# A two-layer hybrid trunk on one core: a list scheduler's engine orders, mLSTM beside RWKV and the output projection, adaLN units moved, sub-layer boundaries by token halves

## The chip, the core and the metric

One Trainium2 chip, one of its cores. The time is device microseconds of one execution of the whole program, a median over runs; smaller is better. The engines named below are PE (TensorE; PEld is its weight load), DVE (VectorE), ACT (ScalarE), POOL (GpSimd) and SP (SyncE, which here issues nearly all DMAs).

## The reference

Two layers with a token mixer and a SwiGLU feed-forward each, for 256 tokens of width 2048 (feed-forward width 5632), all in float32. Each of the four sub-layers computes

```
x <- LayerNorm(ALPHA * x + (1 + gate(c)) * f(x * (1 + scale(c)) + shift(c)))
```

where shift, scale and gate are products of the one conditioning vector `c` with an "adaLN" matrix (2048 x 6144 for each sub-layer). f is, in order:

- layer 0, mixer "ab": one input projection, then eight mLSTM heads (two groups of four) and sixteen RWKV-7 heads (four batches of four), concatenated, then an output projection;
- layer 0, feed-forward: `silu(h Wg) * (h Wu)`, then `Wd`;
- layer 1, mixer "cd": one input projection, then retention and gated DeltaNet (GDN) heads, concatenated, then an output projection;
- layer 1, feed-forward.

RWKV and GDN need the inverse of a small triangular matrix for each head and chunk; mLSTM has a convolution, gates, a weighted score matrix and a norm for each head.

## The kernel before, in words

**Weights.** Nearly every weight is read from HBM once, in units of 1 MB (`raw`, three buffers, issued by SP). Float32 products are made of three float32r matmuls: ACT rounds half a unit into `hi` (L340), DVE subtracts to get `lo` (L341), and PE adds hi·h, lo·h and hi·(rest of h) into a PSUM bank (L360, L361, L362). A unit is four slices of 128 input rows by 512 outputs, so it is 4 slices x 2 token halves (t=0 and t=1, 128 tokens each) x 3 = 24 matmuls of 128x512. `product` (L347 on) runs the units of one block of 512 outputs into two PSUM banks, one for each token half, tag `g`.

**adaLN.** There are 192 `ada_unit`s, 48 for each sub-layer: 1 MB read through the same three `raw` buffers, and one DVE instruction that multiplies by silu(c) and sums along the row (L292). `fill(rate)` puts some of them behind each weight unit of the stages, up to a limit. When a sub-layer's 16 gate columns are there, `gate_rows` (L314) spreads them over all partitions: for each of 16 column blocks a float32 matmul of a broadcast column with the identity (L320, two records each in the profile), and four ACT copies; four times in the program.

**Stages.** `first_products` (the first 164 us) makes the RWKV low-rank columns and three blocks beside 32 adaLN units. `rwkv` runs four batches (`rwkv_batch`, `rwkv_front`, then `rwkv_heads` with `inverses`, then `rwkv_out`), and after each batch issues further blocks of the input projection, which fill PE while DVE works at the heads. The eight blocks that belong to mLSTM (6 to 13) are not used at once: `put_by` copies them out of PSUM (ACT, L705) and stores them in HBM, and `mlstm_group` fetches them later. After RWKV's last batch mLSTM group 0 and then group 1 run, then `mix_out` (the output projection, two halves of four blocks, with `residual` between), then `norm`, `ffn(0)`, `mixer_cd`, `mix_out`, `norm`, `ffn(1)`, `last_norm`.

**Boundaries.** At the end of a sub-layer the last block's banks are multiplied by the gate, added to the residual, and summed (`last_sum`: L483, L484, L485, for each token half), `norm_scales` (L493 to L505) turns the sums into mean and 1/sigma by some twelve DVE instructions of one column, DVE normalises (L522), PE transposes (L527), ACT scales and shifts (L530), and DVE splits (L390, L391) into the next activation `h`. The last unit of the last block has its matmuls ordered by token half (`by_t`), nothing else has.

**What sets the order.** The tile framework's scheduler takes instructions by program order, with offsets: weight loads and splits are 2000 places ahead, the inverses 4000, the norm 3000. Each engine then runs its instructions in that fixed order.

## Time and profile before

| | |
|---|---|
| time of three runs | 2883.45, 2884.39, 2894.77 us; median 2884.39 |
| profiled execution | 2886.5 us, its span 2884.8 us, so 1.7 us lie outside the span |
| mean granted TensorE clock | 0.970 |
| first matmul | 33.8 us; last matmul's end about 2866.3 us |
| first_products | 0 to 164 us |
| RWKV, four batches | 164 to 603 us |
| mLSTM, two groups | 603 to 686 us |
| output projection and norm | 686 to 786 us |
| feed-forward 0 | 786 to 1535 us |
| mixer cd with its output projection | 1535 to 2124 us |
| feed-forward 1 and the last norm | 2124 to 2884.8 us |

The table by stage in the prediction has, for each stretch, its length, the busy time of each engine with its number of records in brackets, the mean granted TensorE clock, the share of time that the DMA engines were busy, and GB/s. A busy PE at a clock of 0.5 does half the work, so idle time and clock have to be read together.

### The profile page before, as it was taken

Reading aid. Unit: us, or ns where it says so; the run is one execution under the profiler, and the core shown is the slowest. Engines: PE = TensorE matmul, PEld = TensorE weight load, DVE = VectorE, ACT = ScalarE, POOL = GpSimd, SP = SyncE. Lnnn points to the kernel's source line nnn. Section 1 sums busy time; section 2 is a strip of 40 time slices with the busy share of each in tenths; the row PEclk is TensorE's granted clock in tenths of the full one; section 3 lists DMA queues with packets and bytes.
Section 4 is the critical chain, followed back from the end, with each engine's and each line's share of the span. In section 5 each row is a group of like instructions: output and inputs, shape, how many; then the busy total and the mean of one; then the engine's idle time right before and its main releaser. Section 6 shows DMA issues by size and latency. Waiting matters only on the chain.

```text
span 2884.8 us, 33590 instructions
## 1 busy us (share of the span) xinstructions
PE 2699.7 (94%) x12746; PEld 2216.1 (77%) x12746; DVE 2035.7 (71%) x3255; ACT 1260.7 (44%) x1663; POOL 73.8 (3%) x88
## 2 busy tenths in 40 slices
PE   3699999987899999999998999999989999999997
PEld 2577788775788888888886778787778888888886
DVE  7888878845876557767758798886876545557556
ACT  2264444435454444444445544344444444443442
POOL 0000000000000000000000010101000000000000
PEclk9799999987999999999999999999999999999998
DMA  9876656632577668867855775667656656656553
GB/s 365 352 270 246 247 187 257 250 123 74 203 259 290 249 228 299 302 229 274 300 196 204 277 280 211 239 252 263 222 194 241 239 192 236 236 219 235 193 218 131
DMA packets 112906, 683.79 MB, mean 237 GB/s; under 512 B 12644, under 2 KB 16872, under 8 KB 35048
## 3 DMA queue, kind: packets, MB, share of 16 engines
q1 hardware_dynamic: 110152, 676.92, 64.1%
q10 hardware_dynamic: 2592, 4.72, 0.4%
q8 instruction: 100, 1.64, 0.2%
q14 instruction: 62, 0.51, 0.0%
HBM read 668.49 MB, written 13.11 MB: 236 GB/s over the span
## 4 chain that ended last, share of the span: by engine, by line
PE 58%; DVE 8%; DMA 4%; issue 1%; ACT 1%; POOL 0%; POOLq 0%; DVEq 0%; ACTq 0%
PE g L361 18%; PE g L362 18%; PE g L360 18%; DVE lo L341 3%; DMA raw<-ada 2%; DVE raw L292 2%; DMA raw<-gu 1%; ACT hi L340 1%; PE m L578 1%; DMA raw<-w_cd 1%; DMA t<-x 1%; PE m L527 0%; PE c L320 0%; PE m L642 0%; PE m L649 0%
## 5 line engine op out<-in xcount | busy, mean ns | idle before, releaser
L341 DVE TENSOR_TENSOR lo<-raw,hi 128x1024 fp32r<-128x1024 f32 (+2 forms) x848 | 1024.2, 1213 | 650.0 <-ACT hi L340 647.5
L340 ACT ACTIVATE hi<-raw 128x1024 fp32r<-128x1024 f32 (+2 forms) x848 | 885.0, 1049 | 1182.4 <-PE g L362 949.5
L360 PE MATMUL g<-hi,h 128*128 128x512 f32 (+3 forms) x2352 | 923.1, 394 | 85.7 <-ACT hi L340 81.0
L361 PE MATMUL g<-lo,h 128*128 128x512 f32 (+3 forms) x2352 | 926.1, 394 | 9.9 <-DVE lo L341 9.6
L362 PE MATMUL g<-hi,h 128*128 128x512 f32 (+3 forms) x2352 | 921.4, 392 | 0.0
L360 PEld LDWEIGHTS g<-hi,h 128*128 128x128 f32 x2352 | 447.3, 191 | 181.2 <-ACT hi L340 85.3
L361 PEld LDWEIGHTS g<-lo,h 128*128 128x128 f32 x2352 | 448.5, 191 | 108.9 <-DVE lo L341 19.9
L362 PEld LDWEIGHTS g<-hi,h 128*128 128x128 f32 x2352 | 447.6, 190 | 88.4 <-issue 3.2
L292 DVE SCALAR_TENSOR_TENSOR raw<-raw,silu_c 128x2048 f32<-128x2048 f32 x176 | 403.1, 2290 | 31.1 <-DMA raw<-ada 30.5
L360 PE MATMUL g<-hi,a 128*128 128x512 f32 x960 | 376.1, 392 | 2.0 <-ACT hi L340 1.1
L361 PE MATMUL g<-lo,a 128*128 128x512 f32 x960 | 375.6, 391 | 2.5 <-DVE lo L341 2.4
L362 PE MATMUL g<-hi,a 128*128 128x512 f32 x960 | 375.7, 391 | 0.0
L361 PEld LDWEIGHTS g<-lo,a 128*128 128x128 f32 x960 | 180.8, 188 | 40.9 <-DVE lo L341 4.0
L360 PEld LDWEIGHTS g<-hi,a 128*128 128x128 f32 x960 | 180.9, 188 | 40.3 <-ACT hi L340 1.6
L362 PEld LDWEIGHTS g<-hi,a 128*128 128x128 f32 x960 | 180.9, 188 | 37.2
L947 DVE SCALAR_TENSOR_TENSOR f<-c,cols_sb,f 128x253 f32<-128x253 f32 (+2 forms) x120 | 53.5, 475 | 13.4 <-ACT f L945 13.1
L530 ACT ACTIVATE t<-m,affine 128x128 f32<-128x128 f32 x96 | 35.0, 474 | 29.9 <-PE m L527 26.4
L1141 POOL TENSOR_SCALAR s<-cons_sb,log_alpha 128x128 f32<-128x128 f32 x16 | 18.1, 1144 | 1065.9 <-DVE log_alpha L1085 895.3
L403 ACT ACTIVATE t<-t,affine 128x256 f32<-128x256 f32 x16 | 8.7, 588 | 76.4 <-DVE affine L301 76.4
L292 DVE SCALAR_TENSOR_TENSOR a<-a,silu_c 128x2048 f32<-128x2048 f32 x16 | 36.6, 2287 | 0.4
L527 PE MATMUL m<-cons_sb,y 128*128 128x128 f32 x96 | 16.9, 319 | 18.4 <-DVE v L495 18.4
L527 PEld LDWEIGHTS m<-cons_sb,y 128*128 128x128 f32 x96 | 13.3, 167 | 23.1 <-issue 20.2
(391 smaller groups left out, 1990.1 us busy)
## 6 DMA issues: line engine op xcount, KB each, us to landing
raw<-ada SPq DMA_DIRECT2D x176, 1024.0 KB, 5.1
raw<-gu SPq DMA_DIRECT2D x176, 1024.0 KB, 4.9
raw<-dn SPq DMA_DIRECT2D x88, 1024.0 KB, 4.8
raw<-w_cd SPq DMA_DIRECT2D x60, 1024.0 KB, 5.1
raw<-w_ab SPq DMA_DIRECT2D x56, 1024.0 KB, 5.5
a<-ada SPq DMA_DIRECT2D x16, 1024.0 KB, 9.6
raw<-o_ab SPq DMA_DIRECT2D x16, 1024.0 KB, 4.9
raw<-o_cd SPq DMA_DIRECT2D x16, 1024.0 KB, 4.8
```

The source lines that it names most:

```text
L292: v.scalar_tensor_tensor(w[:], w[:], 1.0, self.sc[:], ALU.mult, ALU.mult, accum_out=m[:, i:i + 1])
L340: nc.scalar.activation(hi[:, :2 * n], ws, AF.Copy)
L341: nc.vector.tensor_tensor(lo[:, :2 * n], ws, hi[:, :2 * n], ALU.subtract)
L360: mm(o, ah, wh, start=first, stop=False)
L361: mm(o, ah, wl, start=False, stop=False)
L362: mm(o, al, wh, start=False, stop=stop and k == 3)
L403: nc.scalar.activation(h32[:, j, :], x[:, j, :], AF.Identity, bias=self.ab[:, 16 + k:17 + k], scale=self.ab[:, k:k + 1])
L527: nc.tensor.transpose(b[:, P * j:P * j + P], y[t][:, P * k:P * k + P], self.ident)
L530: nc.scalar.activation(h32[:, j, :], b[:, P * j:P * j + P], AF.Identity, bias=self.ab[:, 16 + k:17 + k], scale=self.ab[:, k:k + 1])
L578: nc.tensor.transpose(b[:, P * k:P * k + P], gs[:, t, P * k:P * k + P], self.ident)
L947: v.scalar_tensor_tensor(o[:, d:T], z[:, 0:T - d], self.col(wname, c + 3 - d), o[:, d:T], ALU.mult, ALU.add)
L1141: nc.gpsimd.tensor_scalar(L[:], sl, self.gl[:, t, 4 * g + j:4 * g + j + 1], None, ALU.mult)
```

## The change

1. **A list scheduler in the kernel** (`Plan`, 330 new lines). After the whole program is recorded, it works out each instruction's dependences, gives each a cost by a small table (written in the kernel, with a model of the clock and of one DMA stream), runs a list schedule over the five engines with the old priorities as tie-breaker and the pools' buffer counts as limits, and pins each engine to the order that came out (`impose`), by dependences without a semaphore.
2. **mLSTM beside other work.** `rwkv_heads`, `inverses` and `mlstm_group` become generators. Group 0 is stepped along beside RWKV's last batch (`beside`). Group 1 is handed into `mix_out` as `side` and stepped beside the first half of the output projection; its four blocks (10 to 13) are made there and used straight from PSUM (`direct`), so they are neither stored nor fetched: ACT's `put_by` stores go from 18 to 10.
3. **adaLN units moved.** By stage, before and after: start 32 and 32; RWKV to the first output projection 48 and 48; feed-forward 0 48 and 60; mixer cd 48 and 36; feed-forward 1 16 and 16. After a norm eight weight units pass without one (four before). The scale and shift table keeps all four sub-layers apart.
4. **Gate without PE.** `gate_rows` no longer uses PE or ACT. When a sub-layer's gate is complete, a DMA writes its 128x16 columns transposed into HBM (2048 elements of four bytes), and a second DMA reads the 8 KB row back to all partitions (1 MB). The program has 64 PE matmuls fewer (11775 instead of 11839).
5. **Boundaries by token halves.** The last two units (mixers) or three units (feed-forwards) of a sub-layer's last block run all matmuls of t=0, then all of t=1; the first three units of the next sub-layer do the same. Their split halves live in other pools (`a8`, `q4`, `zt`) so that all are held at once. `norm` takes t=0 to the end before t=1, at a priority of 12000; the normalisation moves from DVE to ACT. `last_norm` goes by halves too.
6. **Small.** Three DVE instructions instead of four for each Newton step of `rsqrt`; in `conv`, `shifted` and `scaled_into` both ACT instructions of a pair are issued before DVE's.

```diff
-    def gate_rows(self):
-        gate = self.y8([P, D])
-        for n in range(4):
-            b = self.bank("c")
-            for j in range(4):
-                k = 4 * n + j
-                self.nc.tensor.matmul(b[:, P * j:P * j + P], self.g1[:, k:k + 1].to_broadcast([P, P]), self.ident, start=True, stop=True)
-            self.nc.scalar.activation(gate[:, 512 * n:512 * n + 512], b[:], AF.Copy)
+        if i == 47:
+            v.scalar_tensor_tensor(self.g1[:], m[:, 32:48], 1.0, self.cols[:, ob + 32:ob + 48], ALU.add, ALU.add)
+            self.gate_row = self.dram.tile([KT, P], F32, name=self.name("gate_row"))
+            nc.sync.dma_start(self.gate_row[:].rearrange("k p -> p k"), self.g1[:])
+
+    def gate_rows(self, room, sub):
+        self.ada(max(0, 48 * sub + 48 - self.ada_next))
+        gate = room([P, D])
+        self.nc.sync.dma_start(gate[:], self.gate_row[:].rearrange("k p -> (k p)").unsqueeze(0).to_broadcast([P, D]))
         return gate
...
+        groups = [(0, head)] + [(i, ("ss",)) for i in range(len(head), m - len(tail))] + [(m - len(tail), tail)]
+        for first, homes in groups:
+            units = range(first, first + len(homes))
+            parts = {i: self.split(srcs[i], n, homes=home) for i, home in zip(units, homes)}
+            if len(homes) == 1:
+                order = [(i, r, t) for i in units for r in range(2) for t in range(NT)]
+            else:
+                order = [(i, r, t) for t in range(NT) for i in units for r in range(2)]
...
+        with self.tc.high_priority(offset=12000):
+            for t, g in ((0, None), (0, 0), (0, 1), (0, 2), (0, 3), (1, None), (1, 0), (1, 1), (1, 2), (1, 3)):
+                if g is None:
+                    self.last_sum(y, banks, 3, stats, [t])
+                    mean, r = self.norm_scales(stats[t])
...
-            if out:
-                out()
-            if i < 4:
-                out = self.rwkv_heads(B)
+            side = beside(i)
+            for _ in self.rwkv_heads(B):
+                next(side, None)
...
-        rate = 48.0 / 80 if l == 0 else 16.0 / 60
+        rate = 64.0 / 84 if l == 0 else 16.0 / 40
...
-        k.mixer_cd(h, 48.0 / 60)
+        k.mixer_cd(h, 32.0 / 44)
...
+        plan = Plan(tc, tc.nc, 250)
+        plan.prepare(0)
+        order, _ = plan.run([x.bass_priority for x in plan.ins])
+        plan.impose(order)
```

What this makes of the order is shown at three places of PE's list. Rows are PE's instructions in order; `xN` is that many of one kind in a row, `g` banks are those of weight products, `m` and `c` banks those of small matmuls.

**First place, the inversions of RWKV's third batch.** Before (L632, L642, L649, L656 are the inversion's matmuls):

```order
L632 MATMUL m_2754<-cons_sb,y_2700 128x128 x4
L362 MATMUL g_3898<-hi_4021,h_674 128x512
L360 MATMUL g_3898<-hi_4021,h_674 128x512
L361 MATMUL g_3898<-lo_4022,h_674 128x512
L362 MATMUL g_3898<-hi_4021,h_674 128x512
L360 MATMUL g_4059<-hi_4063,h_140 128x512
L361 MATMUL g_4059<-lo_4064,h_140 128x512
L362 MATMUL g_4059<-hi_4063,h_140 128x512
L360 MATMUL g_4059<-hi_4063,h_140 128x512
L361 MATMUL g_4059<-lo_4064,h_140 128x512
L362 MATMUL g_4059<-hi_4063,h_140 128x512
L632 MATMUL m_2761<-cons_sb,y_2700 128x128 x4
```

With the change (L1002, L1013, L1020, L1027 are the same matmuls):

```order
L1002 MATMUL m_2750<-cons_sb,y_2696 128x128 x4
L1002 MATMUL m_2757<-cons_sb,y_2696 128x128 x4
L1013 MATMUL m_2763<-y_2696,a_2642 128x64 x4
L1013 MATMUL m_2768<-y_2696,a_2642 128x64 x4
L1161 MATMUL c_3480<-f_3473,cons_sb 128x256
L1020 MATMUL m_2763<-P_2773,y_2696 128x64 x4
L1020 MATMUL m_2768<-P_2775,y_2696 128x64 x4
L1027 MATMUL m_2787<-cons_sb,y_2696 128x128 x4
L1027 MATMUL m_2793<-cons_sb,y_2696 128x128 x4
L1013 MATMUL m_2799<-y_2696,a_2642 128x64 x4
```

Before, weight matmuls (the `g` rows) stand between the inversion's steps; with the change none does for 78 rows, from this batch's first inversion step on, through its heads and into the next batch's first steps (the first ten are shown).

**Second place, mLSTM group 0.** Before, from the second head on (L1000 to L1004 make the weights of a head, L1014 and L1015 its scores, L1041 to L1043 its output):

```order
L1014 MATMUL m_4642<-y_4547 128x256
L1015 MATMUL m_4642<-y_4547 128x128
L1041 MATMUL m_4646<-q_4624,t_4638 128x129
L1042 MATMUL m_4646<-q_4624,t_4638 128x129
L1043 MATMUL m_4646<-q_4624,t_4638 128x129
L1000 MATMUL m_4660<-cons_sb,s_4657 128x256
L1001 MATMUL m_4660<-cons_sb,log_f 128x128
L1002 MATMUL m_4660<-minus_m,cons_sb 128x256
```

With the change, in RWKV's last batch (L1027 is that batch's inversion, L1377 to L1381 are an mLSTM head's weights, L1391 and L1392 its scores):

```order
L1027 MATMUL m_3828<-cons_sb,y_3729 128x128 x4
L1027 MATMUL m_3834<-cons_sb,y_3729 128x128 x4
L1377 MATMUL m_3844<-cons_sb,s_3841 128x256
L1378 MATMUL m_3844<-cons_sb,log_f 128x128
L1379 MATMUL m_3844<-minus_m,cons_sb 128x256
L1380 MATMUL m_3844<-cons_sb,s_3841 128x128
L1381 MATMUL m_3844<-minus_m,cons_sb 128x128
L1391 MATMUL m_3854<-y_3628 128x256
L1392 MATMUL m_3854<-y_3628 128x128
L704 MATMUL g_4599<-hi_4645,h_319 128x512
L705 MATMUL g_4599<-lo_4646,h_319 128x512
L706 MATMUL g_4599<-hi_4645,h_319 128x512
```

Before, one mLSTM head follows another with no weight matmul between; with the change a head stands between the inversion's steps and weight matmuls of the last batch.

**Third place, the boundary from the first mixer to feed-forward 0.** Before (L527 is the norm's transpose):

```order
L361 MATMUL g_5705<-lo_5747,a_5102 128x512
L362 MATMUL g_5705<-hi_5746,a_5102 128x512
L527 MATMUL m_5828<-cons_sb,y_5121 128x128 x4
L360 MATMUL g_5959<-hi_5963,h_5782 128x512
L361 MATMUL g_5959<-lo_5964,h_5782 128x512
L362 MATMUL g_5959<-hi_5963,h_5782 128x512
```

With the change (L884 is the transpose):

```order
L705 MATMUL g_5643<-lo_5659,a_5229 128x512
L706 MATMUL g_5643<-hi_5658,a_5229 128x512
L884 MATMUL m_5742<-cons_sb,y_4211 128x128 x4
L884 MATMUL m_5757<-cons_sb,y_4211 128x128 x4
L884 MATMUL m_5772<-cons_sb,y_4211 128x128 x4
L704 MATMUL g_5899<-q_5903,h_5710 128x512
L705 MATMUL g_5899<-q_5904,h_5710 128x512
L706 MATMUL g_5899<-q_5903,h_5710 128x512
```

In both, no work of another kind stands between the last weight matmul and the first transpose; with the change three of the first half's four transposes stand together, and the 24 matmuls ahead of them all belong to t=1.

More of the change, by code (lines that the diff above doesn't have):

```diff
@@ L364, in product, with part @@
-    def product(self, srcs, n, acts, ada=0.0, by_t=False):
+    def part(self, w, i, n, act, t, bank, start, stop):
+        mm = self.nc.tensor.matmul
+        hi, lo = w
+        ts = slice(P * t, P * t + P)
+        o = bank[:, :n]
+        for j in range(2):
+            k = 2 * i + j
+            ah, al = act[:, 0, k, ts], act[:, 1, k, ts]
+            wh, wl = hi[:, n * j:n * j + n], lo[:, n * j:n * j + n]
+            mm(o, ah, wh, start=start and k == 0, stop=False)
+            mm(o, ah, wl, start=False, stop=False)
+            mm(o, al, wh, start=False, stop=stop and k == 3)
@@ L366, in product, with unit @@
+    def unit(self, src, n, act, banks, start, stop, ahead=2000):
+        parts = self.split(src, n, ahead)
+        for i in range(2):
+            for t in range(NT):
+                self.part(parts[i], i, n, act, t, banks[t], start, stop)
+    def product(self, srcs, n, acts, ada=0.0, head=(), tail=()):
         banks = [self.bank("g") for _ in range(NT)]
         m = len(srcs)
-        for i, s in enumerate(srcs):
-            self.unit(s, n, acts[i], banks, i == 0, i == m - 1, by_t=by_t and i == m - 1)
-            self.fill(ada)
+        groups = [(0, head)] + [(i, ("ss",)) for i in range(len(head), m - len(tail))] + [(m - len(tail), tail)]
[4 more added lines that the diff above has]
+                order = [(i, r, t) for i in units for r in range(2) for t in range(NT)]
+            else:
+                order = [(i, r, t) for t in range(NT) for i in units for r in range(2)]
+            for i, r, t in order:
+                self.part(parts[i][r], r, n, acts[i], t, banks[t], i == 0, i == m - 1)
+            for _ in units:
+                self.fill(ada)
@@ L507, in norm_scales @@
-        return out
-    def norm(self, y, stats, sub):
+        mv, r = self.tiny([P, 2]), self.tiny([P, 1])
+        v.bn_aggr(mv[:], stats[:].rearrange("p (c s) -> p c s", s=6))
+        x, x4, x16, t, u = (self.tiny([P, 1])[:] for _ in range(5))
+        v.tensor_scalar(x, mv[:, 1:2], LN_EPS, None, ALU.add)
+        v.tensor_single_scalar(t.bitcast(I32), x.bitcast(I32), 1, ALU.logical_shift_right)
+        v.tensor_scalar(u.bitcast(I32), t.bitcast(I32), -1.0, float(0x5F3759DF), ALU.mult, ALU.add)
@@ new lines, in norm, with group @@
+        scales = {}
+        def group(t, g):
+            s, ts = slice(512 * g, 512 * g + 512), slice(P * t, P * t + P)
+            mean, r = scales[t]
+            nc.scalar.activation(y[t][:, s], y[t][:, s], AF.Identity, bias=mean, scale=r)
+            b = self.bank()
+            h32 = self.t2([P, 4, P])
+            for j in range(4):
+                k = 4 * g + j
+                nc.tensor.transpose(b[:, P * j:P * j + P], y[t][:, P * k:P * k + P], self.ident)
+            for j in range(4):
+                k = 4 * g + j
+                nc.scalar.activation(h32[:, j, :], b[:, P * j:P * j + P], AF.Identity, bias=self.ab[:, sub + 1, 16 + k:17 + k],
+                                     scale=self.ab[:, sub + 1, k:k + 1])
+                if j % 2:
+                    self.into(acts[g], ts, h32[:, j - 1:j + 1, :], slice(j - 1, j + 1))
@@ new lines, in norm @@
+        with self.tc.high_priority(offset=12000):
+            for t, g in ((0, None), (0, 0), (0, 1), (0, 2), (0, 3), (1, None), (1, 0), (1, 1), (1, 2), (1, 3)):
+                if g is None:
+                    self.last_sum(y, banks, 3, stats, [t])
+                    mean, r = self.norm_scales(stats[t])
+                    off = self.tiny([P, 1])
+                    v.scalar_tensor_tensor(off[:], mean, -1.0, r, ALU.mult, ALU.mult)
+                    scales[t] = off[:], r
+                else:
+                    group(t, g)
@@ L567, in ffn @@
                 u0 = (l * NFB + j) * 8
-                banks = self.product([gu[u0 + i] for i in range(4)], 512, h, rate)
+                banks = self.product([gu[u0 + i] for i in range(4)], 512, h, rate, head=HEAD if j == 0 else ())
                 gs = self.q4([P, NT, 512])
@@ L584, in ffn @@
             if third == 1:
-                self.gate = self.gate_rows()
+                self.gate = self.gate_rows(self.y8, sub)
             for n in range(4):
                 u0 = l * 44 + d0 + n * m
-                banks = self.product([dn[u0 + i] for i in range(m)], 512, a, 0.0, by_t=third == 2 and n == 3)
+                banks = self.product([dn[u0 + i] for i in range(m)], 512, a, 0.0, tail=FFN_TAIL if third == 2 and n == 3 else ())
                 if third == 0:
@@ L1326, in product @@
             at[0] += KG
-            return self.product([w[u + i] for i in range(KG)], 512, h, rate)
+            return self.product([w[u + i] for i in range(KG)], 512, h, rate, head=() if u else HEAD)
         def gates():
```

582 lines of the change are left out of this document (445 added, 137 removed).

## The prediction

> **What bounds the kernel now.** I read the busy times first, then the chain that ended last, then a table by stage, then the waits at the seams.
>
> ```profile
> span 2884.8 us, 33590 instructions
> PE 2699.7 (94%) x12746; PEld 2216.1 (77%) x12746; DVE 2035.7 (71%) x3255; ACT 1260.7 (44%) x1663; POOL 73.8 (3%) x88
> PEclk9799999987999999999999999999999999999998
> PE 58%; DVE 8%; DMA 4%; issue 1%; ACT 1%; POOL 0%; POOLq 0%; DVEq 0%; ACTq 0%
> PE g L361 18%; PE g L362 18%; PE g L360 18%; DVE lo L341 3%; DMA raw<-ada 2%; DVE raw L292 2%; DMA raw<-gu 1%; ACT hi L340 1%; PE m L578 1%; DMA raw<-w_cd 1%; DMA t<-x 1%; PE m L527 0%; PE c L320 0%; PE m L642 0%; PE m L649 0%
> ```
>
> PE is busy 94% of the span, the three weight matmuls alone are 54% of the chain. So no reordering can do much in the long stages; only what PE idles, or runs at a lower clock, can be won. Where that is, the table by stage tells (stretch, length, then busy time of PE, PEld, DVE, ACT and POOL with records, granted clock, DMA share, GB/s):
>
> ```profile
> 164.00:260.00 96.00, 91.94 (x419) 69.65 (x418) 85.44 (x175) 55.19 (x90) 4.32 (x5) 1.00 0.75 277
> 260.00:360.00 100.00, 96.23 (x537) 78.10 (x536) 80.79 (x203) 48.23 (x86) 4.60 (x6) 1.00 0.65 234
> 360.00:461.00 101.00, 99.85 (x552) 81.26 (x550) 81.75 (x206) 50.06 (x90) 5.86 (x5) 0.98 0.60 222
> 461.00:564.00 103.00, 97.36 (x522) 78.76 (x520) 82.65 (x196) 44.64 (x78) 4.93 (x6) 0.97 0.67 243
> 564.00:686.00 122.00, 95.52 (x478) 75.18 (x476) 58.57 (x168) 51.86 (x91) 11.62 (x22) 0.77 0.29 104
> 686.00:786.00 100.00, 92.74 (x430) 76.18 (x431) 78.44 (x160) 51.45 (x68) 1.22 (x3) 0.96 0.47 169
> 786.00:1535.50 749.50, 740.54 (x3320) 610.59 (x3318) 509.36 (x557) 322.03 (x353) 0.00 (x0) 0.99 0.71 261
> 1535.50:1726.00 190.50, 175.75 (x880) 144.15 (x881) 162.77 (x335) 101.93 (x163) 14.98 (x12) 0.96 0.72 261
> 1726.00:1852.00 126.00, 120.31 (x639) 100.39 (x638) 108.63 (x248) 51.82 (x82) 14.74 (x15) 0.97 0.61 225
> 1852.00:2124.50 272.50, 258.62 (x1283) 213.47 (x1281) 214.88 (x362) 116.33 (x155) 11.21 (x10) 1.00 0.66 238
> 2124.50:2866.40 741.90, 740.38 (x3320) 612.51 (x3320) 432.14 (x457) 318.97 (x349) 0.00 (x0) 0.99 0.59 216
> ```
>
> Idle PE time plus (1 - clock) times the length is what a stretch loses at most: 4, 4, 3, 9, 55, 11, 17, 22, 10, 14 and 9 us, 158 in all. Over a third lies in one stretch, 564 to 686 us, where RWKV's last batch ends and the mLSTM groups run:
>
> ```profile
> 564.00:603.00 39.00, 38.93 (x285) 35.38 (x283) 19.24 (x31) 13.77 (x23) 2.97 (x6) 1.00 0.62 223
> 603.00:650.00 47.00, 36.18 (x129) 27.13 (x129) 20.74 (x70) 19.52 (x35) 3.36 (x7) 0.69 0.17 61
> 650.00:686.00 36.00, 20.41 (x65) 12.67 (x65) 18.59 (x69) 18.58 (x34) 5.29 (x10) 0.64 0.09 30
> ```
>
> From 603 us on PE has few records, the clock falls to 0.64, and DVE is not full either: a chain of small steps with nothing beside it. It loses (47 - 36.2) + 0.31 x 47 + (36 - 20.4) + 0.36 x 36 = 54 us of 83, or 0.65 us for each unfilled us.
>
> **The change, part by part.** All sums are made against the profiled execution (2884.8 us span and 1.7 outside it, 2886.5), and the difference is then taken from the median of the runs, 2884.39, which lies 2 us under it.
>
> *Gate off PE.*
>
> ```profile
> L320 PE MATMUL c<-cons_sb,one_and_gate 128*128 128x128 f32 x128 | 18.0, 286 | 0.9 <-DVE f L947 0.9
> q1 hardware_dynamic: 110152, 676.92, 64.1%
> q10 hardware_dynamic: 2592, 4.72, 0.4%
> ```
>
> The 128 records were busy 18.0 us; each of the 16 bursts ends with some 0.15 us that the next instruction overlaps (0.286 of a record less the 18.0 / 128 = 0.14 between two), so PE gets at most 18.0 - 16 x 0.15 = 15.6 us back; some bursts stand where PE had slack, so **-15**. In its place come four DMAs of 2048 four-byte elements, on SP's queue ahead of weight units: SP waits there for DVE's last adaLN sum, and the read-back for the write; queued behind are raw units, for which ACT, DVE and then PE wait. The trace has no DMA like it. From below: q10's packets of 1.8 KB took 0.004 x 16 x 2884.8 / 2592 = 0.07 us and q1's of 6.1 KB 0.641 x 16 x 2884.8 / 110152 = 0.27 us, so time goes with bytes and 128 tiny ones on each of 16 engines take at most 128 x 0.07 = 9 us. From above, 0.27 us each makes 34 us. Three raw units are loaded ahead, each 24 matmuls long, and the matmuls follow each other by 0.226 us:
>
> ```profile
> 774.64 0.39 PE L360 MATMUL g<-hi,a 128*128 128x512 f32 x1
> 774.86 0.39 PE L361 MATMUL g<-lo,a 128*128 128x512 f32 x1
> 775.09 0.39 PE L362 MATMUL g<-hi,a 128*128 128x512 f32 x1
> ```
>
> so a unit lasts 5.4 us and the buffers cover 16. Nine us vanish under them; 34 would stick out by 18, four times 72. I take the nearer row (q10's small packets): **+1**. By the Trainium skill ("DMA: Bandwidth & Descriptors", Specifications) a transfer needs 512 bytes or more for line rate, and below that the engine reads, modifies and writes; with the 0.2 us HBM access of its section "Latency and other measured facts" an estimate is 128 x 0.2 = 26 us, which would stick out by 10 us, four times. No run here shows it yet.
>
> *mLSTM beside other work.* The four blocks 10 to 13 are 4 x 4 units x 5.4 = 87 us of weight matmuls that before filled RWKV's last batches and now stand beside mLSTM group 1 and the output projection; group 0 stands beside the last batch's inversion. If all of 603 to 686 were filled, the 54 us would be won. But the blocks are missing where they were: in the changed order the third batch's inversion and heads stand without weight matmuls. A batch is some 100 us (rows 360 to 564), with DVE busy 82 of them, of which about half is inversion and heads. 40 us unfilled, at the rate measured above, lose 0.65 x 40 = 26. Bounds: 54 won, or nothing. I take 54 - 26, rounded down to **-25**. Eight stores and eight fetches fewer of 256 KB count nothing, under ACT's 56% of idle time; were ACT the bound, the copies ahead of the stores would be 8 x 0.6 us.
>
> *Boundaries.*
>
> ```profile
> PE m L527 <- DVE v L495: 18.4, 3, 6.2
> 779.20:785.70 6.50, 0.36 (x2) 0.02 (x1) 6.33 (x22) 1.16 (x2) 0.00 (x0) 0.91 0.46 161
> 785.70:795.00 9.30, 8.00 (x35) 5.95 (x36) 7.59 (x29) 4.54 (x13) 0.00 (x0) 0.70 0.59 226
> L530 ACT ACTIVATE t<-m,affine 128x128 f32<-128x128 f32 x96 | 35.0, 474 | 29.9 <-PE m L527 26.4
> L483 DVE TENSOR_TENSOR t<-g,y 128x512 f32<-128x512 f32 x32 | 20.9, 682 | 4.3 <-PE g L362 4.3
> L705 ACT ACTIVATE sp<-g 128x512 f32<-128x512 f32 x18 | 10.8, 598 | 26.2 <-DMA by<-sp 17.7 <-PE g L362 5.0 <-PE m L632 3.2
> ```
>
> Three times PE waits 6.1 us for the norm, then 1.3 us for the first activations, then runs at a clock of 0.70 for 9.3 us (2.8 more): 10 us each. With the change the chain for t=0 (three sums of 0.68, some twelve column operations, normalise, transpose: about 6 us without the splits and the other half's sums that stood between) lies under t=1's matmuls: 24 x 0.226 = 5.4 us at a mixer's end, 36 x 0.226 = 8.1 at a feed-forward's. Late next is ACT: four normalisations of 0.6 (L705 has the same size) and 16 x 0.474 make 10 us for a half, against 8.1 us of the next stage's t=0 matmuls. So some 4 us stay: 10 - 4 = 6, three times, **-18** (bounds 0 and -30).
>
> ```profile
> 2866.30:2884.80 18.50, 0.05 (x1) 0.00 (x0) 14.92 (x43) 0.00 (x0) 0.00 (x0) 0.60 0.31 113
> ```
>
> At the very end 18.5 us follow the last matmul, 14.9 of them DVE for both halves. One half's scales and 8 output passes now go under 8.1 us of matmuls: **-5** (bounds 0 and -8).
>
> *adaLN moved.*
>
> ```profile
> L292 DVE SCALAR_TENSOR_TENSOR raw<-raw,silu_c 128x2048 f32<-128x2048 f32 x176 | 403.1, 2290 | 31.1 <-DMA raw<-ada 30.5
> ```
>
> Twelve units leave the cd mixer: 12 x 2.29 = 27.5 us of DVE and 12 MB. There DVE is busy 163 of 190.5, 109 of 126 and 215 of 272.5 us, and the three rows lose 22 + 10 + 14 = 46. The list order helps in the same place. I take two thirds of the DVE time: **-18** (bounds 0 and -35). They go into feed-forward 0, where DVE has 240 us free and the DMAs move 261 GB/s; 12 MB more make 277, a rate the first row of the table shows without loss. Raw buffers are shared, so a few splits come later: **+2** (bounds 0 and 20, the latter if a unit's read shows once in each of the 12).
>
> *The rest.*
>
> ```profile
> 33.80:160.00 126.20, 86.39 (x368) 72.55 (x369) 101.43 (x130) 41.43 (x54) 0.10 (x1) 0.82 0.87 338
> ```
>
> The first stage moves 338 GB/s with PE idle for 40 of 126 us: it waits for bytes, of which the change moves none, so nothing. The four RWKV rows lose 20 us that a better list order may reach; I count nothing, since the third batch was charged above. Shorter `rsqrt` chains and paired ACT issues: nothing, PE's products cover them.
>
> Sum: -15 + 1 - 25 - 18 - 5 - 18 + 2 = **-78**; 2884.4 - 78 = **2806 us**.
>
> **The rivals.**
>
> *Nearly all is won.* The list order fills the third batch from elsewhere and the waits go: 15 (gate) + 45 of 54 + 35 in cd + 27 at the boundaries + 8 at the end + 9 in RWKV = 139, **2745 us**. For it: DVE has room everywhere (71% of the span). Against it: the 78 rows without a product.
>
> *The third batch starves, mLSTM wins nothing.* Group 0's small steps now compete with the last batch's inversion for DVE and each waits for the other: -25 becomes 0 to +5, **2834 us**. For it: the slow rows 603 to 686 have no engine full, so latency, not work, is their price, and latency stays where nothing else is issued. By the Trainium skill ("TensorE: Matmul & The Clock Gate", "Why this matters for your kernels") PE gaps over about 3 us bring half clock; the trace agrees, with 0.70 after the gap of 6.5 us.
>
> *The gate row holds the queue.* 34 us each, less 16 of cover: 2806 + 72 = **2878 us**, no change.
>
> *Slower: an imposed order that is wrong about durations.*
>
> ```profile
> PE g L361 <- DVE lo L341: 12.0, 19, 1.7
> ```
>
> The list is made from costs in the kernel; where a real time differs, an engine waits in front of a ready instruction. PE's order goes from weight matmuls to small ones some 250 times (counted in the order). A wait like this row's, 12.0 / 19 = 0.63 us, at each is 157 us: **2963 us**. It decides from 78 / 250 = 0.31 us a hand-over on. Against it: the order before was fixed as well, with as many hand-overs, and lost only 158 us in all the stretches.
>
> **How the numbers follow.** Forecast 0.53, nearly all won 0.17, starved 0.15, gate row 0.07, slower 0.08. What a measurement can tell from no change is about 0.5%, 14 us. The first three are faster, the fourth is the same: faster 0.85, same 0.07, slower 0.08. The range of 2745 to 2855 reaches from the full gain over the starved case (2834) and half of the gate row's wait (2842); outside it are the slower case, most of the gate row's, and a little below.
>
> **What would show it.** Right: no L320 rows; in the waits no 6 us before the transposes but 2 to 4; clock over 0.9 where mLSTM runs; a stretch near 450 to 500 us with a low clock and few PE records (the third batch); DVE's share in cd down by some 27 us; feed-forward 0 still about 749 us long. Wrong: raw units landing tens of us late after the last adaLN unit of a sub-layer; PE idle before small matmuls in hundreds of places; feed-forward 0 longer by over 10 us.

## The result: 0.75% faster, where 2.7% was forecast

The changed kernel takes 2864.53 us (median of five runs, 2860.3 to 2870.13), beside 2885.55 us for the kernel before: a ratio of 0.9925, with a 95% interval of 0.9903 to 0.9947. That is 21 us, where 78 were forecast; the range (2745 to 2855) does not hold it. Differences between kernels below are taken from their ratios to the kernel before, times 2885 us, so that runs made at different times can be set side by side.

The page of the changed kernel, its first lines and its packets:

```profile
span 2868.4 us, 33238 instructions
PE 2701.2 (94%) x12618; PEld 2215.9 (77%) x12618; DVE 2024.6 (71%) x3189; ACT 1261.6 (44%) x1668; POOL 69.3 (2%) x88
PE 60%; DMA 10%; DVE 10%; ACT 3%; issue 1%; POOL 0%; ACTq 0%; DVEq 0%; SPq 0%
DMA packets 118664, 683.80 MB, mean 238 GB/s; under 512 B 20708, under 2 KB 23912, under 8 KB 40296
```

PE is busy as long as before (2701 us against 2700) although it has 128 records fewer: by the trace's clock records 132 us of that busy time lie where the clock was 0.5, 97 us before. DMA's share of the chain went from 4% to 10%.

The table by stage of the changed kernel, with edges at the same events as before (the first step of each inversion, the first transpose of each norm):

```profile
271.50:388.50 117.00, 107.79 (x537) 87.95 (x536) 80.80 (x198) 48.36 (x85) 3.78 (x6) 0.90 0.61 197
388.50:492.10 103.60, 94.68 (x522) 75.80 (x520) 82.70 (x204) 47.95 (x87) 3.69 (x5) 0.97 0.63 227
492.10:581.30 89.20, 81.75 (x384) 67.22 (x385) 52.22 (x175) 39.38 (x80) 7.38 (x11) 0.71 0.21 72
581.30:780.00 198.70, 193.42 (x989) 158.02 (x987) 155.54 (x324) 106.13 (x154) 11.71 (x20) 0.99 0.55 201
780.00:1546.60 766.60, 745.77 (x3280) 606.68 (x3280) 532.41 (x574) 321.69 (x357) 0.00 (x0) 0.99 0.75 273
1546.60:1731.60 185.00, 173.33 (x884) 146.53 (x885) 150.15 (x318) 102.99 (x167) 13.02 (x12) 0.96 0.69 240
1731.60:1852.20 120.60, 116.89 (x638) 99.02 (x637) 105.74 (x236) 51.28 (x82) 12.22 (x13) 0.99 0.60 221
1852.20:2114.60 262.40, 254.86 (x1258) 212.09 (x1256) 200.26 (x340) 117.68 (x156) 9.95 (x11) 0.99 0.64 229
2114.60:2852.30 737.70, 734.91 (x3288) 605.73 (x3288) 433.36 (x464) 317.40 (x349) 0.00 (x0) 1.00 0.61 218
```

Against the table before, the late stages moved as they should: mixer cd is 21 us shorter (568 against 589), the last feed-forward 4. The stretch with mLSTM (581 to 780) is at a clock of 0.99 with PE busy 97%. But layer 0's mixer as a whole ends at 780.0 instead of 785.7, only 6 us earlier, and feed-forward 0 is 16 us longer. In this table two rows are worse than the same batches before the change: by idle time and clock, counted as in the prediction, the first inversion's batch (117 us long, clock 0.90) loses 21 us instead of 4, and the third's (clock 0.71) 33 instead of 9.

Two places show what happens. The first, at the end of the adaLN units of feed-forward 0, in the timeline of the changed kernel (start, length, engine, line; in brackets the idle time before and what ended it):

```profile
954.18 0.39 SPq L655 DMA_DIRECT2D gate_row<-one_and_gate  x1
...
957.35 1.77 SPq L667 DMA_DIRECT2D raw<-gu  x1
...
972.71 2.00 ACT L689 ACTIVATE hi<-raw 128x1024 fp32r<-128x1024 f32 x2 [12.80 <-DMA raw<-gu]
...
973.82 0.79 PE L704 MATMUL g<-hi,h 128*128 128x512 f32 x1 [6.33 <-ACT hi L689]
```

and the same stretch in pieces of 4 us (the last column is GB/s, the third from the end the clock):

```profile
954.00:958.00 4.00, 3.12 (x13) 1.94 (x12) 2.52 (x3) 2.94 (x3) 0.00 (x0) 1.00 0.87 311
958.00:962.00 4.00, 4.00 (x19) 3.34 (x18) 1.88 (x2) 1.06 (x1) 0.00 (x0) 1.00 0.44 18
962.00:966.00 4.00, 3.79 (x17) 2.80 (x17) 2.63 (x3) 0.00 (x0) 0.00 (x0) 1.00 1.22 57
966.00:970.00 4.00, 1.49 (x7) 0.89 (x5) 0.00 (x0) 0.00 (x0) 0.00 (x0) 0.97 0.41 59
970.00:974.00 4.00, 0.18 (x1) 0.18 (x1) 0.20 (x1) 1.29 (x2) 0.00 (x0) 0.50 0.98 391
```

After the 8 KB gate write the core's DMAs move 18 to 59 GB/s for 12 us, and a weight unit issued in that time lands 15 us later. PE's loaded work lasts until 967, then it stands 6.3 us and comes back at half clock. The other three writes are held in the same way (279, 1624 and 2469 us): PE stands 5.9 us after the first and 6.0 after the third, and not at all after the fourth. The second place is the third batch:

```profile
492.00:557.00 65.00, 58.56 (x290) 48.51 (x290) 28.74 (x98) 20.57 (x52) 6.25 (x10) 0.66 0.09 33
```

65 us with no weight read to speak of (33 GB/s), a clock of 0.66 and 290 PE records.

### The profile page after: what moved, and what is told of

It is laid out like the page before. It is cut to its first block, busy times and chain, and to the rows that moved or that the text cites. A ratio compares the mean times of both kernels' runs of the same rounds, so it can differ in the third digit from the quotient of the medians.

```text
span 2868.4 us, 33238 instructions
## 1 busy us (share of the span) xinstructions
PE 2701.2 (94%) x12618; PEld 2215.9 (77%) x12618; DVE 2024.6 (71%) x3189; ACT 1261.6 (44%) x1668; POOL 69.3 (2%) x88
## 4 chain that ended last, share of the span: by engine, by line
PE 60%; DMA 10%; DVE 10%; ACT 3%; issue 1%; POOL 0%; ACTq 0%; DVEq 0%; SPq 0%
PE g L705 18%; PE g L706 18%; PE g L704 18%; DMA raw<-gu 4%; DVE lo L690 3%; DVE raw L634 3%; DMA raw<-ada 2%; ACT hi L689 2%; DMA raw<-w_cd 1%; PE m L1013 1%; PE m L1020 1%; PE m L948 1%; DMA t<-lnrow 1%; DMA raw<-w_z 0%; PE m L1027 0%
## 5 line engine op out<-in xcount | busy, mean ns | idle before, releaser
L690 DVE TENSOR_TENSOR lo<-raw,hi 128x1024 fp32r<-128x1024 f32 (+3 forms) x826 | 994.3, 1212 | 612.0 <-ACT hi L689 608.6
L689 ACT ACTIVATE hi<-raw 128x1024 fp32r<-128x1024 f32 (+3 forms) x826 | 859.5, 1048 | 1232.5 <-PE g L706 854.6
L704 PE MATMUL g<-hi,h 128*128 128x512 f32 (+3 forms) x2304 | 907.5, 395 | 81.2 <-ACT hi L689 53.6
L705 PE MATMUL g<-lo,h 128*128 128x512 f32 (+3 forms) x2304 | 908.9, 395 | 18.0 <-DVE lo L690 17.6
L706 PE MATMUL g<-hi,h 128*128 128x512 f32 (+3 forms) x2304 | 903.2, 393 | 0.0
L704 PEld LDWEIGHTS g<-hi,h 128*128 128x128 f32 x2304 | 440.0, 191 | 176.3 <-ACT hi L689 58.9
L706 PEld LDWEIGHTS g<-hi,h 128*128 128x128 f32 x2304 | 439.9, 191 | 85.1 <-issue 1.3
L704 PE MATMUL g<-hi,a 128*128 128x512 f32 x920 | 360.3, 392 | 6.8 <-DVE t L845 5.4
L705 PE MATMUL g<-lo,a 128*128 128x512 f32 x920 | 360.5, 392 | 0.8 <-DVE lo L690 0.8
L706 PE MATMUL g<-hi,a 128*128 128x512 f32 x920 | 359.8, 391 | 0.0
L704 PEld LDWEIGHTS g<-hi,a 128*128 128x128 f32 x920 | 173.2, 188 | 43.8 <-DVE t L845 6.1
L706 PEld LDWEIGHTS g<-hi,a 128*128 128x128 f32 x920 | 173.3, 188 | 35.8 <-DVE a L748 0.5
L1184 PE MATMUL m<-y 64*128 64x256 f32 x128 | 31.1, 454 | 2.2 <-DVE a L1187 1.9
L951 ACT ACTIVATE a<-m 128x512 fp32r<-128x512 f32 x44 | 26.0, 591 | 14.8 <-PE m L948 13.5
```

Of the source, the lines that this page charges most:

```text
L689: nc.scalar.activation(hi[:, :2 * n], ws, AF.Copy)
L690: nc.vector.tensor_tensor(lo[:, :2 * n], ws, hi[:, :2 * n], ALU.subtract)
L704: mm(o, ah, wh, start=start and k == 0, stop=False)
L705: mm(o, ah, wl, start=False, stop=False)
L706: mm(o, al, wh, start=False, stop=stop and k == 3)
L1184: mm(b[:, T * x:T * x + T], bk[r, c, x, t, :], ar[r, c, t].rearrange("p x s -> p (x s)"), start=True, stop=True)
```

## The experiments

The theory (A): the scattered gate write costs some 30 us, and the list's order starves the third batch. The rivals: the write is harmless and the denser adaLN reads make the waits; or the list's order is a gain that something else eats.

**The gate turned on PE.**

```diff
-            nc.sync.dma_start(self.gate_row[:].rearrange("k p -> p k"), self.g1[:])
+            b = self.bank("c")
+            nc.tensor.transpose(b[:KT, 0:P], self.g1[:], self.ident)
+            turned = self.t1([P, P])
+            nc.scalar.activation(turned[:KT, :], b[:KT, 0:P], AF.Copy)
+            nc.sync.dma_start(self.gate_row[:], turned[:KT, :])
```

> The changed kernel, but the gate's 128x16 columns are first turned on PE (one 128x16 transpose, one ACT copy of 16x128) and written to HBM as 16 rows of 512 bytes instead of 2048 elements of 4 bytes. Theory A (the scattered write holds the DMA engines for about 12 us each time, and PE stands for 6 us and then runs at half clock): the four writes cost some 30 us in all, 2864 - 30 = about 2835 us, and the stretch with under 60 GB/s after each write is gone. Rival (the write is harmless, the waits there come from the denser adaLN reads): within 5 us of 2864.

Measured: 2829.37 us, ratio 0.982 (0.9798 to 0.9841), 30 us faster than the changed kernel by the ratios. In its trace 8128 packets are gone (the four writes had 4 x 2048 and now have 4 x 16), and the pieces after the write of feed-forward 0, issued at 943.4, keep their rate:

```profile
DMA packets 110536, 683.80 MB, mean 241 GB/s; under 512 B 12516, under 2 KB 15784, under 8 KB 32168
947.00:951.00 4.00, 4.00 (x19) 3.34 (x18) 3.97 (x6) 1.61 (x2) 0.00 (x0) 1.00 0.64 217
951.00:955.00 4.00, 4.00 (x19) 3.30 (x19) 3.21 (x6) 1.26 (x2) 0.00 (x0) 1.00 0.82 324
```

So the write was the wait, not the denser reads.

**No list scheduler.** The four lines that build and pin the order are left out.

> The changed kernel without the list scheduler: everything else stays, and the framework's own scheduler orders the engines by the same priorities. Theory A (the list's order is worth something, the rest of the change eats it): slower than the changed kernel, 2875 to 2900 us. Rival (the imposed order is what costs, since real times differ from its costs): faster than the changed kernel, below 2855 us.

Measured: 2832.95 us, ratio 0.9832 (0.9803 to 0.986), 27 us faster than with the list. The rival was right, and my belief that the list's order must be worth something fell. The scattered write is still there in this kernel.

**The list scheduler alone**, on the kernel before.

> The kernel before with the list scheduler alone, nothing else changed. Theory A (the list recovers waits of the mLSTM and cd stretches only): 2850 to 2875 us, about 10 to 35 us under the kernel before. Rival (an imposed order costs): 2885 us or more.

Measured: 2877.72 us, ratio 0.9978 (0.9966 to 0.9989): 6 us, less than theory A's 10 to 35. So on the old program the list is a small gain, on the new one a loss. In its trace mixer cd is 11 us shorter (577.5 against 588.7) and layer 0 hardly changes.

**Two more blocks stored.**

```diff
         def direct(i, out):
+            if i < 2:
+                return spilled(4 + i, out)
             banks = product(10 + i)
-            if i < 2:
-                return self.by_tokens(banks)
...
-            for _ in range((0, 1, 3, 0)[i]):
+            for _ in range((0, 1, 5, 0)[i]):
```

> The changed kernel, but blocks 10 and 11 (mLSTM group 1's q and k) are stored to HBM after RWKV's third batch and fetched later, as before the change; only v and o come straight from PSUM. Theory A (the third batch has no weight matmuls because a direct block's copy needs one of two zt buffers, which group 0's fetched columns hold): weight matmuls stand in the third batch's inversion again, its stretch of 65 us at a clock of 0.66 is gone, and the time falls by 15 to 25 us, to about 2843 us. Rival (the stretch is long because of DVE's small steps, and the matmuls only move): within 5 us of 2864.

Measured: 2876.83 us, ratio 0.9978 (0.9963 to 0.9992), 15 us slower than the changed kernel. Both were wrong. The third batch and the stretch with mLSTM after it:

```profile
496.60:593.50 96.90, 79.86 (x469) 64.96 (x467) 79.45 (x211) 47.40 (x89) 8.71 (x11) 0.92 0.56 201
593.50:791.50 198.00, 191.47 (x882) 159.77 (x882) 126.67 (x293) 94.26 (x142) 10.19 (x20) 0.87 0.38 135
```

The third batch has weight matmuls again and its clock rose from 0.71 to 0.92, but the last stretch fell from 0.99 to 0.87: the matmuls that fill one stretch are missing in the other. The number of weight matmuls beside RWKV and mLSTM is fixed; here, under the list, putting them elsewhere moved the hole and did not close it.

**Both cures**: gate turned, no list.

> Both at once: the gate turned on PE and written in 512-byte rows, and no list scheduler. Theory A (two separate losses, the scattered write and the list's order): if they add up 2864.5 - 35.1 - 31.6 = 2798 us; the framework's order shows less after the writes than the list's (excess over PE's own work in feed-forward 0 18.6 us against 36.4), so rather 2805 to 2815. Rival (the list only hurt because it met the slow write, so that one cure does for both): no faster than either alone, 2829 to 2833.

Measured: 2816.54 us, ratio 0.977 (0.9745 to 0.9794): 66 us under the kernel before. The two losses are separate, and each makes the other larger: the write costs 18 us without the list (0.9832 against 0.977) and 30 with it; the list costs 27 us with the write and 14 without. By stage, in us from the traces (edges as above; one execution each, which for the changed kernel and for the gate turned took 6 and 9 us more than the median, so only differences of several us count):

| | before | changed | gate turned | no list | both |
|---|---|---|---|---|---|
| start to the first norm | 785.7 | 780.0 | 769.9 | 748.5 | 749.2 |
| feed-forward 0 | 750.3 | 766.6 | 754.3 | 750.9 | 745.5 |
| mixer cd | 588.7 | 568.0 | 558.5 | 574.2 | 567.2 |
| feed-forward 1 to the last matmul | 741.6 | 737.7 | 738.0 | 736.4 | 735.8 |
| after it | 18.4 | 16.1 | 15.9 | 15.8 | 15.8 |

The write costs in three places of four (10, 12 and 10 us with the list, 0, 5 and 7 without); in feed-forward 1 the write is held too, but PE does not wait after it. The list loses 21 us in layer 0's mixer and 9 in feed-forward 0, and wins 9 in cd. The 21 us are there already at RWKV's first inversion: with the gate turned it starts at 270.4 us under the list and at 247.1 under the framework's order, after 490 instead of 405 PE records on the weight banks. What is done earlier there shortens nothing later: from that inversion to the norm it takes 499.5 us under the list and 502.1 without. The list alone on the kernel before starts it late too (273.2 against 259.9).

**Without the token halves**, on the kernel with both cures: `HEAD`, `MIX_TAIL` and `FFN_TAIL` are empty.

> As the kernel with the gate turned and without the list, but the last units of a block and the first units of the next stage go through their matmuls as all other units do (t=0 and t=1 of each half unit in turn), no split halves are held in other pools; the norm still takes t=0 before t=1. Theory A (the halves give 6 us at each of three boundaries and 5 at the end, as forecast): 20 to 25 us slower than with them. Rival (the order of the norm alone, t=0 first, gives most of it): less than 8 us slower.

Measured: 2838.8 us, ratio 0.9848 (0.9821 to 0.9876), 22.5 us slower, as theory A has it. But this is not what the halves gain over the kernel before. There PE waited 18.4 us for the norms, in three waits (the first L527 row in the prediction). Its waits in front of the same transposes here, without the halves and then with them, and last in the changed kernel, which has the list:

```profile
PE m L888 <- ACT y L883: 34.1, 6, 6.2
```

```profile
PE m L888 <- ACT y L883: 15.9, 4, 6.5
```

```profile
L884 PE MATMUL m<-cons_sb,y 128*128 128x128 f32 x96 | 15.3, 282 | 6.1 <-ACT y L879 5.8
```

With the norm taken by halves and the matmuls not, PE waits six times, so the kernel without the halves is worse at these places than the kernel before. Idle time and low clock together, from 15 us before the first transpose of each of the three norms to 45 after it, are 37 us in the kernel before, 55 without the halves, 26 with them under the framework's order, and 12 in the changed kernel.

**The old adaLN rates**, on the same kernel: 48/80 to unit 128, 48/60, 16/60 and a pause of four.

> As the kernel with the gate turned and without the list, but adaLN units at their places of before: 48 in feed-forward 0, 48 in mixer cd, four units of pause after a norm. Theory A (12 units fewer free DVE in cd, as forecast): feed-forward 0 faster by 2 us or so, cd slower by 18, together 10 to 20 us slower. Rival (DVE is not what cd waits for): within 5 us.

Measured: 2836.95 us, ratio 0.984 (0.9813 to 0.9867), 20 us slower. Theory A. Its two first stretches of cd, against those with the new rates (the second pair):

```profile
1490.10:1675.10 185.00, 172.24 (x846) 142.77 (x847) 152.49 (x317) 100.95 (x162) 10.81 (x11) 0.94 0.67 251
1675.10:1813.80 138.70, 131.35 (x683) 109.31 (x682) 112.95 (x246) 56.39 (x89) 15.81 (x16) 0.96 0.60 220
```

```profile
1494.70:1669.60 174.90, 168.05 (x869) 140.93 (x870) 143.99 (x313) 100.88 (x165) 17.81 (x12) 0.98 0.66 243
1669.60:1796.10 126.50, 122.89 (x652) 103.19 (x651) 106.31 (x239) 52.79 (x84) 12.09 (x15) 0.97 0.60 222
```

10 and 12 us shorter, with 15 us less DVE; feed-forward 0 took 744.6 with the old rates and 745.5 with the new.

**The list is told of the write.** In its cost table the four writes take 12 us of the DMA stream; the write itself stays scattered.

```diff
+                if self.bytes[i] == 8192.0:
+                    self.bytes[i] = 12000 * 358.0
```

> The changed kernel, scattered write and list scheduler both kept, but the list's cost table is told that each of the four writes takes 12 us of the DMA stream. Theory A (the order is built on a wrong duration, so engines stand in front of work that waits for late reads): part of the 35 us comes back, 2840 to 2855 us. Rival (the DMA engines' 12 us are lost however the order stands): within 5 us of 2864.

Measured: 2844.09 us, ratio 0.9869 (0.9846 to 0.9892), 16 us faster than the changed kernel. Theory A: about half of what the write costs with the list comes from an order that was built on a wrong duration. At the first write the changed kernel shows one such place. DVE's list has an adaLN sum next, whose read is held by the write, and two steps of the inversion (L1023) behind it, on which PE's next matmuls wait:

```profile
286.46 0.33 SPq L667 DMA_DIRECT2D raw<-ada  x1
...
300.38 2.29 DVE L634 SCALAR_TENSOR_TENSOR raw<-raw,silu_c 128x2048 f32<-128x2048 f32 x1 [6.21 <-DMA raw<-ada]
...
302.60 0.75 DVE L1023 TENSOR_TENSOR y<-m,y 128x256 f32<-128x256 f32 x2
...
303.08 1.97 PE L1027 MATMUL m<-cons_sb,y 128*128 128x128 f32 x8 [5.89 <-DVE y L1023]
```

With the list told, PE waits at most 2.0 us there, yet the first batch is no shorter (118.6 us against 117.0); feed-forward 0 is 8 us shorter and layer 0's mixer 9, in its second batch and its last stretch. That one duration is all that was changed, but how it reaches those stages is not shown.

**mLSTM after RWKV**, on the kernel with both cures: all eight blocks are stored, both groups run after RWKV's last batch.

> As the kernel with the gate turned and without the list (2816.5 us), but mLSTM as before the change: all eight of its blocks are stored to HBM in RWKV, and both groups run after RWKV's last batch and ahead of the output projection. Theory A (the interleaving of mLSTM is a gain of about the forecast's 25 us once nothing else eats it): 20 to 30 us slower, about 2841 us, the loss between the last inversion and the output projection. Rival (the third batch loses what mLSTM wins, so it gives nothing by itself): within 6 us.

Measured: 2825.65 us, ratio 0.9784 (0.9755 to 0.9812), 4 us slower, less than these runs can tell apart (the intervals overlap; they leave no room for 25). The rival: interleaving mLSTM gives little or nothing under the framework's order. Four stretches from the first inversion to the first norm, first with mLSTM after RWKV, then interleaved:

```profile
247.90:344.70 96.80, 93.94 (x530) 76.39 (x529) 78.99 (x195) 48.80 (x86) 3.84 (x6) 1.00 0.67 240
344.70:442.00 97.30, 96.09 (x536) 78.44 (x536) 81.44 (x199) 49.92 (x90) 5.24 (x5) 1.00 0.65 239
442.00:545.30 103.30, 100.67 (x556) 82.34 (x555) 85.25 (x199) 44.67 (x79) 6.12 (x6) 1.00 0.72 257
545.30:745.80 200.50, 175.55 (x898) 141.63 (x897) 144.64 (x317) 102.78 (x159) 13.85 (x25) 0.96 0.47 170
```

```profile
247.10:346.80 99.70, 95.81 (x530) 77.75 (x529) 79.25 (x195) 50.19 (x87) 3.84 (x6) 0.98 0.65 232
346.80:448.30 101.50, 97.50 (x536) 79.59 (x536) 81.64 (x199) 49.30 (x90) 6.02 (x5) 0.98 0.65 240
448.30:541.30 93.00, 89.00 (x497) 72.46 (x496) 75.70 (x203) 47.18 (x90) 7.92 (x11) 0.96 0.51 178
541.30:749.20 207.90, 193.94 (x957) 158.95 (x956) 151.50 (x312) 98.12 (x146) 12.63 (x20) 0.94 0.51 188
```

497.9 us in all with mLSTM after RWKV, 502.1 interleaved. The earlier batches are fuller when the blocks stay there, the last stretch is fuller when they go there. Yet both end the stage some 40 us earlier than the kernel before (745.8 and 749.2 against 785.7). Something else in the change had done that. Some 12 us of it lie ahead of the first inversion, which starts at 247.9 and 247.1 instead of 259.9; what makes these was not measured.

**The place of RWKV's last output step**, on the kernel just shown. Before the change `rwkv_out` of the fourth batch stood between mLSTM's groups; the change moves it ahead of both, a line of the diff that I had not priced.

```diff
-            last = B
+            last = self.last_batch = B
             side = beside(i)
             for _ in self.rwkv_heads(B):
                 next(side, None)
-            if i == 3:
-                self.rwkv_out(last)
             finish(side)
...
         finish(self.mlstm_group(0, spilled))
+        self.rwkv_out(self.last_batch)
         finish(self.mlstm_group(1, spilled_too))
```

> As the kernel with mLSTM after RWKV (2825.7 us), but RWKV's last output step (rwkv_out of the fourth batch) stands between mLSTM's two groups, as it did before the change, instead of ahead of both. Theory A (layer 0's mixer is some 36 us shorter than before because this step's chain of small DVE instructions no longer collides with mLSTM group 0's, where PE stood 7.6 and 6.0 us and then ran at half clock): 15 to 25 us slower, about 2845 us. Rival (the shorter chains of rsqrt and the paired ACT instructions did it, wherever the step stands): within 6 us.

Measured: 2841.77 us, ratio 0.9863 (0.983 to 0.9897), 23 us slower than with the step ahead of mLSTM. Theory A; from the first inversion to the first norm this kernel takes 522.1 us, near the 525.8 of the kernel before. PE's waits in the last stretch show the two gaps of the kernel before (first fence) again where the step stands between the groups (second), and not where it stands ahead (third):

```profile
PE m L958 <- DVE q L1062: 8.1, 2, 7.4
...
PE c L875 <- ACT t L870: 5.7, 1, 5.7
```

```profile
PE m L1337 <- issue: 7.2, 2, 6.7
PE c L1254 <- ACT t L1249: 5.8, 1, 5.8
```

```profile
PE g L708 <- DVE t L849: 6.2, 1, 6.2
PE m L888 <- ACT y L883: 5.3, 1, 5.3
PE m L1395 <- ACT y L1330: 4.7, 1, 4.7
```

Of the waits that stand there, the first two are the boundary's (the kernel of the second fence has them too, 4.8 and 5.3 us), the third is a step of mLSTM.

**The list with its early half block held back**, gate turned.

```diff
...
+        plan.deps[held].add(first)
```

(`held` is the first matmul of block 6, `first` the first transpose of the first inversion.)

> The changed kernel with the gate turned and with the list, but the first matmul of block 6 may not be listed before the first inversion's first transpose; so the half block that the list takes early (48 rows of PE's list) stays for later batches. Theory A (the list is 13 us slower than the framework's order, 2829.4 against 2816.5, because it spends weight matmuls ahead of the first inversion and the third batch then has none): 2815 to 2820 us, the third batch's excess over PE's own work down from 28.7 us to about 10. Rival (the matmuls are lost elsewhere, or the list's other places cost): 2829 us within 5.

Measured: 2830.85 us, ratio 0.9799 (0.9774 to 0.9823), against 0.982 (0.9798 to 0.9841) without the hold: the intervals overlap, and it does not reach the 0.977 of the framework's order. RWKV's third batch is at a clock of 0.94 now (0.76 with the gate turned and no hold), as theory A had it, but the first two are at 0.93 and 0.90 (1.00 and 0.90 without the hold): the hole moved once more. By the total time theory A fell. The first inversion still starts at 264.2 us, 17 later than under the framework's order, with 432 instead of 405 PE records on the weight banks ahead of it. Why the list still loses some 14 us with the write cured is shown by place (ahead of the first inversion, and in feed-forward 0), not by cause.

**The better of each**: gate turned, the framework's order up to the end of feed-forward 0, the list's order pinned from mixer cd on.

> The gate turned on PE, the framework's order up to the end of feed-forward 0, the list's order pinned only from mixer cd on. Theory A (the list's order is worse in RWKV and feed-forward 0 and better in cd, as the traces with and without it show: 769.9 + 754.3 against 749.2 + 745.5 us, then 558.5 against 567.2): the better of each, 5 to 10 us under 2816.5, about 2809 us. Rival (what cd wins with the list depends on the state in which the list enters it): within 4 us of 2816.5, or slower.

Measured: 2803.99 us (2801.59 to 2810.66), ratio 0.9732 (0.9703 to 0.9762), 11 us under both cures alone by the ratios (the two intervals overlap, 0.9745 to 0.9794 there) and 77 us under the kernel before. The time is theory A's, its mechanism is not shown: the trace (an execution 7 us above the median) has mixer cd at 563.9 us against 567.2, 3 us of the 9 expected, and layer 0's mixer, where the order is the framework's in both, is 4 us shorter as well (745.5 against 749.2).

## Why the prediction was wrong

**The step that failed first: "Nine us vanish under them", the +1 for the gate row.** Its price was 18 us without the list and 30 with it. The hold of about 12 us for each write lay near the lower bound (9), far below the upper (34); what was wrong is the cover. I counted three raw buffers as three weight units, 16 us. adaLN units go through the same three buffers, and a unit issued behind the write needs its own 5 us after it: in the fence above PE ran out 9 us after the rate fell, the unit issued behind the write landed after 15, and the difference is the gap of 6 us. Under the list three of the four writes made such a gap (5.9, 6.3 and 6.0 us), 18 us, and the low clock after each came on top. The rival with the held queue named the mechanism and was given 0.07. The Trainium skill ("DMA: Bandwidth & Descriptors", Specifications) warned in the right direction, that transfers under 512 bytes do not run at line rate; the traces agree for this write, 8 KB that cost 12 us, and show more: the weight read behind it fell to 18 to 59 GB/s as well. The estimate of 26 us drawn from it was twice the measured hold.

**The second: the list's order was taken to help in cd and at the boundaries and to cost nothing elsewhere.** Where help was expected it did help: 9 us in cd, and 10 us less wait in front of the norms' transposes (6.1 against 15.9). But the prediction put nothing on the other side, and in layer 0 the first inversion starts 23 us later under the list. Alone it gave 6 us, in the changed program it cost 27. The rival "an imposed order that is wrong about durations" was right in kind, with a chance of 0.08: telling the list one duration gave 16 us back. Its argument against, that the order before was fixed as well, was true, and did not bear on what a wrong duration does to the order.

**The third batch: right in kind, the size with some luck.** Forecast were 40 us without weight matmuls at 0.65 us lost for each, 26 us, and a low clock near 450 to 500 us. The trace has 65 us from 492 to 557 at a clock of 0.66, which lose at most 6.4 + 0.34 x 65 = 28 us: longer, but 0.43 us for each. It is the list's doing: with both cures the batch has a clock of 0.96.

**mLSTM: the right size by luck.** Layer 0's mixer was to give 25 us beside the gate and its boundary. With both cures it ends 36.5 us earlier in all. But the interleaving gives 4 us, within what can be told; 23 us come from the moved `rwkv_out` (measured with mLSTM after RWKV), which the prediction did not price, and 12 lie ahead of the first inversion. The sum there took 54 us as won and 26 as lost; with a fixed number of weight matmuls to fill with, the runs show the two about even.

**Boundaries: right in kind, the agreement of the size is luck.** Forecast were 10 us each before and "some 4 us stay", 18 won in all. In the changed kernel PE's waits at the first boundary, from the transposes to the second weight unit, add up to 4.7 us, and by idle time and low clock the three boundaries won some 25 us (37 to 12). Under the framework's order they won 11. So the list's order has a large part in what the boundaries gave, and the 22.5 us measured without the halves agree with the forecast 23 because the kernel without them is worse there than the one before. The end took 16 us after the last matmul instead of 18.4 (19.8 without the halves): 2 us of the 5.

**adaLN: right.** Forecast -18 + 2, measured -20, and feed-forward 0 pays about 1 us. DVE's busy time in cd fell by 30 us in the changed kernel, forecast were some 27. Feed-forward 0 was to stay near 749 us; it does (745.5) with both cures, and was 766.6 with neither.

**Gate off PE, -15:** not measured alone. The L320 bursts are gone in all the kernels with the change. That PE's busy time did not fall in the changed one is the clock: counted at full clock (the 97 and 132 us at half clock taken as half), it fell from 2651 to 2635 us, 16 us.

Taken together: the terms that were about the change's own work (gate -15, halves -23, adaLN -16, layer 0 -25) make 79, and the kernel with both cures measures 66. That these are near each other is in part luck, since mLSTM and the halves brought less than their terms and the moved `rwkv_out` stood in no term. The 45 us between that kernel and the changed one are the write and the list.

## What to carry to other kernels

Before an 8 KB transfer is called free, count its elements: a scattered write of 2048 four-byte elements held this core's DMAs to 18 to 59 GB/s for 12 us, and with one transpose on PE, which made 16 rows of it, that hold was gone. An engine order built from a cost table is as good as its worst duration, so compare it with the framework's order on the chip, stage by stage, and pin it only where it wins. When something is taken out to see what it was worth, look whether what is left is worse than the start (here, the norm by halves without the matmuls by halves). And when filler is fixed, moving it beside one idle stretch can open another: price both ends, and look at the unpriced lines of a diff (here, a step moved ahead of another) before a gain is put down to the change's headline.

## What the runs showed of the hardware

Small matmuls did not hold the clock up in the third batch (492 to 557 us), even where PE hardly waited. PE was busy 58.6 of 65 us, and the granted clock was 0.66. It was at half in three parts: 485 to 512, 530 to 540 and 543 to 564 us. The first had begun ahead of the batch, with a wait for the split of a weight unit:

```profile
485.94 0.80 PE L704 MATMUL g<-hi,h 128*128 128x512 f32 x1 [3.81 <-ACT hi L689]
```

The second followed 17 us at full clock, in which PE's longest wait was 1.1 us:

```profile
512.40:529.50 17.10, 15.75 (x125) 14.24 (x125) 3.50 (x10) 8.04 (x17) 0.00 (x0) 1.00 0.00 1
529.50:539.70 10.20, 9.64 (x39) 7.42 (x38) 5.86 (x28) 2.15 (x8) 0.00 (x0) 0.50 0.00 0
```

The Trainium skill ("TensorE: Matmul & The Clock Gate", "Why this matters for your kernels") asks for no PE gaps over about 3 us; here, by the trace, the first fall agrees, with a gap of 3.8 us, and at the second, gaps of at most 1.1 us did not keep the clock. What share of busy time would, no run here isolates.

The hold after the scattered write is longer than its elements: by the trace's packets all 2048 were read within some 2 us, and the low rate lasted 10 us more: packets of 8 KB behind them, which took 0.31 us elsewhere, took 1 to 5 us each. Whether the HBM side or the four-byte size makes that, the runs do not tell apart, since the turned write changed both the element size and the count.
